# Matmul operand tiles moved to multiples of 1024 bytes, with a later first norm and a later sum for k

## The chip, the core and the metric

The kernel runs on one core of a Trainium2 chip. The metric is device time in microseconds (us) of one execution. A core has TensorE (PE; its weight loads are listed as PEld), VectorE (DVE), ScalarE (ACT), GpSimd (POOL) and a queue engine (SP) that issues most DMAs. TensorE multiplies a stationary tile by a moving tile of up to 512 columns and accumulates in PSUM. SBUF is the on-chip memory that holds both; an address here is a byte offset that is the same in each of its 128 partitions.

## The reference

One layer of a decoder trunk, for 256 tokens of width 2048, in float32:

```python
h = rmsnorm(x, norm_mix)
z = h @ w_in                      # 9472 columns, split into nine parts
hq, hf, hi, hgate, aq, ak, av, g_hg, g_at = jnp.split(z, offsets, axis=-1)
y_hg = (rmsnorm(hgrn2(hq, hf, hi, lower), hg_norm) * silu(hgate)) @ w_hg_out
qa, ka = rmsnorm(aq, q_norm), rmsnorm(ak, k_norm)      # per head
y_at = swa_sinks(qa, ka, av, sinks) @ w_at_out         # window 128
x = x + (sigmoid(g_hg) * y_hg + sigmoid(g_at) * y_at) @ w_out
h2 = rmsnorm(x, norm_ffn)
x = x + square(relu(h2 @ w_up)) @ w_down
```

## The kernel before

All weights are streamed once, as 250 chunks of 1 MiB (128 partitions x 2048 float32). A chunk is worked on in two halves, and the program is written as one long loop over half chunks, called ticks: tick 2i and 2i+1 belong to chunk i. The order of everything is written by hand: `at_pe(t, f)` and `at_post(t, f)` put f behind the main matmuls of tick t, `finish` puts an evacuation at a tick, and each engine executes its instructions strictly in the order in which the loop wrote them.

A float32 product is made of three products of rounded operands (`float32r`). For each half, ScalarE writes `hi`, the rounded copy of the chunk's half (`split_hi`, three ticks ahead), and VectorE writes `lo`, the remainder (`split_lo`, two ticks ahead). The activations have the same two parts. Two forms of half chunk follow:

- "one" (`mm_part`): 8 matmuls with hi stationary and both parts of an activation as 512 moving columns, then 8 with lo stationary and 256 moving columns. The input projection (activation `hT`; chunks 4 to 41, so 76 halves) and the up projection (`h2`; 64 chunks, 128 halves) have this form.
- "tok" (`mm_tok`): 12 matmuls with an activation stationary and 512 columns of hi or lo moving. The gates (32 chunks), the mixing (16), the output projection (16) and the down projection (64) have this form: 128 chunks of 24 matmuls, 3,072 in all.

The program starts with chunks 0 to 3 in quarters: 16 units of 4 + 4 matmuls (`start_split`, tiles `shi`/`slo`), fed by 1 MiB quarters of x (`xs`) and of the four chunks as they land. Behind these, SP's queue has x by tokens (`x_tok`, two DMAs of 1 MiB), chunk 4 (`raw4`), the constants, and chunks 5 and 6. ScalarE squares x by tokens with a running sum (`squares`), `norm_tok` makes the reciprocal root and two diagonal tiles `dg`, and TensorE sums them with ones into `rstd` (`norm_pe`, behind tick 9), which all evacuations of the input projection multiply by. Later `qknorm` norms q and k of the attention the same way: square, remainder (`nl`), a sum on TensorE (`nps`), a root. For k these are asked for from tick 68 on, the sum behind tick 70.

In the built program the first pool, `base`, holds small tiles of odd sizes and then the large ones, and all that follows is shifted by them. The tiles of the main matmuls begin at these places: `hT` (later `mixT` and half of `u`) at byte 21,472, which is 992 over a multiple of 1024; `xs` (later `oact` and the other half of `u`) also 992 over one; `raw`, `hi`, `lo`, `h2`, `shi`, `slo` all 32 over one. The identity in `consts`, the moving operand of every transpose, begins 384 over one. Every slice that a matmul moves or holds is a multiple of 512 bytes further on, and one of 512 columns is 2048 bytes long.

Of the kernel before, what the change touches and what calls it, by code (L numbers as in the profile page):

```python
# [10 lines left out]
F32 = mybir.dt.float32  # L11
# [7 lines left out]
P = 128  # L19
T = 256  # L20
# [22 lines left out]
def trunk_kernel(  # L43
# [14 lines left out]
    nc = tc.nc  # L58
    ctx.enter_context(tc.manual_schedule())

    base = ctx.enter_context(tc.tile_pool(name="base", bufs=1))
    raws = ctx.enter_context(tc.tile_pool(name="raws", bufs=4))
    split = ctx.enter_context(tc.tile_pool(name="split", bufs=3))
    ev = ctx.enter_context(tc.tile_pool(name="ev", bufs=2))
    psm = ctx.enter_context(tc.tile_pool(name="psm", bufs=4, space=PSUM))
    pss = ctx.enter_context(tc.tile_pool(name="pss", bufs=4, space=PSUM))

# [12 lines left out]
    S_END = len(chunks)  # L80
    AHEAD = 3
    N_START = 4
    T_START = 11
    START_LEAD = 4

    params = base.tile([P, P_W], F32, name="params")
    consts = base.tile([P, C_W], F32, name="consts")
    cr = base.tile([P, R_W], F32R, name="cr")
    rstd = base.tile([P, T], F32, name="rstd")
    lb = base.tile([P, HG_HEADS], F32, name="lb")  # L90
    omlb = base.tile([P, HG_HEADS], F32, name="omlb")
    kn8 = base.tile([P, 1], F32, name="kn8")

    ident = consts[:, C_ID : C_ID + P]
    ones = cr[:, R_ONES : R_ONES + P]
# [9 lines left out]
    def load(i):  # L105
        if i < S_END:
            raw_of[i] = raws.tile([P, KT, P], F32, tag="raw", name=f"raw{i}")
            nc.sync.dma_start(raw_of[i], chunks[i])
# [87 lines left out]
    def at_pe(s, f):  # L196
        pe_side.setdefault(s, []).append(f)

    def at_post(s, f):
        post.setdefault(s, []).append(f)  # L200
# [1 line left out]
    acts = {}  # L202

    def new_act(key, tag):
        acts[key] = base.tile([P, KT, 2, T], F32R, tag=tag, name=key)
        return acts[key]

    hT = new_act("hT", "A")

    xs = base.tile([P, KT, 2, T], F32, tag="C", name="xs")  # L210
    xv = xs[:, :, 0, :]
    xtok = xs[:, :, 1, :]

# [16 lines left out]
    def load_w(i, q):  # L230
        nc.sync.dma_start(raw0[i][:, 4 * q : 4 * q + 4, :], chunks[i][:, 4 * q : 4 * q + 4, :])
# [6 lines left out]
    for q in range(1, 4):  # L238
        load_x(4 * q, 4 * q + 4)
        for i in range(N_START):  # L240
            load_w(i, q)
    for t in range(2):
        nc.sync.dma_start(xtok[:, 8 * t : 8 * t + 8, :], x_tok[t].rearrange("p (m c) -> p m c", m=8))
    load(N_START)
    nc.sync.dma_start(cr0, csr)
    nc.sync.dma_start(consts, cst)
    load(N_START + 1)
    load(N_START + 2)

    def x_part(lo, hi):  # L250
# [44 lines left out]
        nc.tensor.matmul(ps, lhsT=lhsT, rhs=hi, start=True, stop=False)  # L295
        nc.tensor.matmul(ps, lhsT=lhsT, rhs=lo, start=False, stop=True)

    r1 = base.tile([P, 2], F32, name="r1")
    sm = base.tile([P, 3, 2], F32, name="sm")
    dg = base.tile([P, 2, 2, P], F32R, name="dg")  # L300

    def norm_tok(total_sq, r):
        v, q = sm[:, 1, :], sm[:, 2, :]
        nc.vector.tensor_scalar(v, total_sq, 1.0 / D, EPS, ALU.mult, ALU.add)
# [22 lines left out]
        part = xtok[:, 8 * t : 8 * t + 8, :]  # L327
        nc.scalar.activation(part, part, AF.Square, accum_out=sm[:, 0, t : t + 1])  # L328

    at_post(6, lower_bounds)  # L330
    at_post(6, lambda: squares(0))
    at_post(7, lambda: squares(1))
    at_post(7, constants)
    at_post(8, lambda: norm_tok(sm[:, 0, :], r1))
    at_pe(9, lambda: norm_pe("1"))
    at_post(10, lambda: norm_post("1"))

    evac = {}

# [296 lines left out]
    at_pe(2 * S_AV + 4, avpe)  # L636
    at_post(2 * S_AV + 5, avpost)

    def qknorm(s, z, gain, n, name):
        st = {}  # L640

        def new(m, dt=F32):
            return hg["pool"].tile([P, 512], dt, tag="g2", bufs=9, name=m)[:, 0:n]

        def a():
            sq, hi = st["sq"], st["hi"] = new(f"nq_{name}"), new(f"nh_{name}", F32R)
            nc.scalar.activation(hi, z, AF.Square)
            nc.gpsimd.tensor_mul(sq, z, z)

        def a2():  # L650
            st["lo"] = new(f"nl_{name}", F32R)
            nc.vector.tensor_sub(st["lo"], st["sq"], st["hi"].bitcast(F32))

        def b():
            st["ps"] = psum_side(f"nps_{name}")
            sums(st["ps"][:, 0:n], blk64, st["hi"], st["lo"])

        def c():
            st["v"] = mean_eps(st["ps"][:, 0:n], 64, new(f"nv_{name}"))

        def c2():
            st["r"] = rsqrt_start(st["v"], new, f"n{name}")

        def d():
            r = rsqrt_finish(*st["r"])
            nc.vector.scalar_tensor_tensor(z, z, gain, r, ALU.mult, ALU.mult)

        at_post(s, a)
        at_post(s + 1, a2)
        at_pe(s + 2, b)  # L670
        at_post(s + 3, c)
        at_post(s + 4, c2)
        at_post(s + 5, d)

    halves = (slice(0, 64), slice(64, P))

# [15 lines left out]
        for n, own in enumerate(halves):  # L692
            nc.vector.tensor_sub(t[halves[1 - n], n, :], aqz[own, j, :], t[own, n, :].bitcast(F32))

    qknorm(68, akz, kn8, T, "k")
    at_post(T_GATES, stack_k)
    for j, t in enumerate((74, 78, 82, 85)):
        qknorm(t, aqz[:, 2 * j : 2 * j + 2, :].rearrange("p j t -> p (j t)"), qng, 512, f"q{j}")
# [1 line left out]
    def pair(j, s):  # L700
# [20 lines left out]

        def a2():
            sc = pool().tile([P, 2, 384], F32, tag="sc", name=f"sc_{j}")
            mx = pool().tile([P, 2, 2], F32, tag="mx", name=f"mx_{j}")
            for n, h in enumerate(heads):
                nc.vector.scalar_tensor_tensor(
                    sc[:, n, :],
                    dist,
                    float(np.float32(2.0 ** (-8.0 * (h + 1.0) / AT_HEADS))),
                    st["ps"][n][:, 0:384],  # L730
                    ALU.mult,
                    ALU.add,
                )
            nc.vector.tensor_reduce(mx[:, :, 0:1], sc[:, :, 0:P], AX.X, ALU.max)
            nc.vector.tensor_reduce(mx[:, :, 1:2], sc[:, :, P:384], AX.X, ALU.max)
            for n, h in enumerate(heads):
                nc.vector.tensor_scalar(
                    mx[:, n, :], mx[:, n, :], params[:, P_SINK + h : P_SINK + h + 1], -1.0, ALU.max, ALU.mult
                )
            st.update(sc=sc, mx=mx)  # L740

        def b():
            sc, mx = st["sc"], st["mx"]
            sm = pool().tile([P, 2, 2], F32, tag="sm", name=f"sm_{j}")
            es = pool().tile([P, 2, 2], F32, tag="es", name=f"es_{j}")
            for n, h in enumerate(heads):
                for q, sl in enumerate((slice(0, P), slice(P, 384))):
                    nc.scalar.activation(
                        sc[:, n, sl], sc[:, n, sl], AF.Exp, bias=mx[:, n, q : q + 1], accum_out=sm[:, n, q : q + 1]
                    )  # L750
                nc.scalar.activation(es[:, n, :], mx[:, n, :], AF.Exp, bias=params[:, P_SINK + h : P_SINK + h + 1])
            st.update(sm=sm, es=es)
# [236 lines left out]
    for tick in range(2 * S_END + 2):  # L989
        i, odd = divmod(tick, 2)  # L990
        if not odd:
            if i >= N_START:
                load(i + AHEAD)
            for key, tag in fresh.get(i, ()):
                new_act(key, tag)
        if tick == 2 * N_START:
            to_hgrn()
        if tick == T_GATES:
            to_gates()
        if tick == 2 * S_OUT + 3:  # L1000
            open_ff()
        split_hi(ticks[tick + 3])
        split_lo(ticks[tick + 2])
        for f in due.pop(tick, ()):
            f()
        h = ticks[tick]
        i, odd = divmod(h, 2)
        if i < N_START:
            for n in (2 * tick, 2 * tick + 1):
                j, q = units[n]  # L1010
                if q == 0:
                    start_ps.append(psum_main(j) if j < 2 else psum_side(f"mm{j}"))
                mm_part(start_ps[j], hT, 4 * q, *start_w.pop(n), q == 0, q == 3)
                start_split(n + START_LEAD)
                if q == 3:
                    finish(jobs[j][2], 1, T_START + j // 2, start_ps[j], j)
        elif i < S_END:
            kind, act, ef = jobs[i][:3]
            if kind == "tok":
                k0, first, last = jobs[i][3:]  # L1020
                first, last = first and not odd, last and odd == 1
                if first:
                    main_ps["tok"] = [psum_main(f"{h}_{t}") for t in range(2)]
                ps = main_ps["tok"]
                mm_tok(ps, act(), k0 + 2 * odd, hi_of.pop(h), lo_of.pop(h), first, last)
            else:
                if not odd:
                    main_ps[i] = psum_main(h)
                ps = main_ps[i]
                mm_part(ps, act(), 8 * odd, hi_of.pop(h), lo_of.pop(h), not odd, odd == 1)  # L1030
            t0 = tick + 1 + 2 * (i in (S_FF, S_FF + 1))
            if i < N_START + 4:
                t0 = max(t0, T_START + i // 2)
            if S_G <= i < N_IN:
                t0 = max(t0, T_GATES + 1)
            finish(ef, odd, t0, ps, i)
        for f in post.get(tick, []):
            f()
        for f in pe_side.get(tick, []):
            f()  # L1040
# [98 lines left out]
```

## Time and profile before

| what | us |
|---|---|
| time, median of 3 runs (1372.82 to 1374.32) | 1372.89 |
| the profiled execution, its own time | 1372.77 |
| its span, first to last instruction | 1371.0 |
| TensorE busy in it | 1350.6 |
| VectorE busy | 852.0 |
| ScalarE busy | 686.3 |
| GpSimd busy | 188.6 |

Times inside the trace count from the span's start. A row of the timeline gives the start and the length of a run of equal instructions; matmuls overlap, so the pace of a series is read from the start of one run to the start of the next, not from the length of one matmul.

### The profile page before, as it was taken

The page shows a single profiled execution, that of the slowest core. Times are in us where ns is not written, and L with a number is a line of the kernel's source. Part 1 is how long each engine was busy: PE and PEld are TensorE (multiplying, and loading weights), DVE is VectorE, ACT ScalarE, POOL GpSimd, SP SyncE. Part 2 cuts the span into 40 slices and gives each one's busy share as a digit, 9 for nine tenths or more (in the row PEclk, how much of TensorE's full clock was granted, in tenths as well). Part 3 has the DMA queues.
Part 4 walks back from the last instruction along what each step waited for, and adds up shares of the span by engine and source line. Part 5 has one row for each costly group of instructions (what it writes and reads, how often), then busy time and mean ns, then how long its engine had stood idle before and what let it go on. Part 6 is the DMA issues. An engine that isn't in the chain of part 4 may idle for free.

```text
span 1371.0 us, 17892 instructions
## 1 busy us (share of the span) xinstructions
PE 1350.6 (99%) x6912; PEld 1140.1 (83%) x6912; DVE 852.0 (62%) x1067; ACT 686.3 (50%) x976; POOL 188.6 (14%) x181
## 2 busy tenths in 40 slices
PE   7999998999999999999999999999999999999998
PEld 6888887888888888888888888888888888888887
DVE  4688889795666466655666665444456666644443
ACT  5856656566665634454644444333344444443432
POOL 0334535310000001000111110000001111100000
PEclk9999999999999999999999999999999999999999
DMA  9554554455544555665555555555555555556661
GB/s 342 200 182 150 185 184 144 153 189 167 175 157 162 177 187 181 210 225 182 183 187 192 196 190 187 186 192 199 190 184 187 186 193 193 193 185 202 212 214 47
DMA packets 42453, 255.40 MB, mean 186 GB/s; under 512 B 4480, under 2 KB 8704, under 8 KB 12928
## 3 DMA queue, kind: packets, MB, share of 16 engines
q1 hardware_dynamic: 42224, 254.23, 54.1%
q8 instruction: 54, 0.88, 0.2%
q14 instruction: 31, 0.25, 0.1%
q10 hardware_dynamic: 144, 0.03, 0.0%
HBM read 252.15 MB, written 2.10 MB: 185 GB/s over the span
## 4 chain that ended last, share of the span: by engine, by line
PE 90%; DVE 4%; DMA 2%; issue 1%; POOL 1%; ACT 1%; SPq 0%; DVEq 0%; POOLq 0%; ACTq 0%
PE mm L129 23%; PE mm L153 17%; PE mm L151 17%; PE mm L152 17%; PE mm L137 12%; DMA raw<-w_in_t 1%; DVE lo L120 1%; DVE lf L418 1%; DMA xs<-xT 0%; POOL vT L342 0%; POOL lfb L404 0%; PE pt L767 0%; PE po L782 0%; PE s L713 0%; ACT xs L328 0%
## 5 line engine op out<-in xcount | busy, mean ns | idle before, releaser
L120 DVE TENSOR_TENSOR lo<-raw,hi 128x1024 fp32r<-128x1024 f32 x460 | 582.4, 1268 | 435.3 <-PE mm L152 266.4
L114 ACT CAST hi<-raw 128x1024 fp32r<-128x1024 f32 x460 | 482.5, 1050 | 608.8 <-PE mm L153 358.7
L129 PE MATMUL mm<-h,hi 128*128 128x512 f32 x1024 | 256.5, 392 | 0.0
L129 PEld LDWEIGHTS mm<-h,hi 128*128 128x128 f32 x1024 | 184.3, 189 | 33.1
L153 PE MATMUL mm<-hi,u 128*128 128x512 f32 x512 | 201.7, 394 | 0.0
L152 PE MATMUL mm<-lo,u 128*128 128x512 f32 x512 | 200.7, 392 | 0.0
L151 PE MATMUL mm<-hi,u 128*128 128x512 f32 x512 | 198.7, 388 | 0.0
L129 PE MATMUL mm<-hT,hi 128*128 128x512 f32 x608 | 156.3, 399 | 0.0
L137 PEld LDWEIGHTS mm<-h,lo 128*128 128x128 f32 x1024 | 139.7, 190 | 10.0
L137 PE MATMUL mm<-h,lo 128*128 128x256 f32 x1024 | 142.8, 282 | 0.0
L123 POOL CAST u<-s 128x256 fp32r<-128x256 f32 x64 | 60.3, 943 | 565.3 <-ACT s L930 565.3
L129 PEld LDWEIGHTS mm<-hT,hi 128*128 128x128 f32 x608 | 109.7, 189 | 21.0
L152 PEld LDWEIGHTS mm<-lo,u 128*128 128x128 f32 x512 | 96.1, 188 | 22.4
L151 PEld LDWEIGHTS mm<-hi,u 128*128 128x128 f32 x512 | 96.1, 188 | 21.4
L153 PEld LDWEIGHTS mm<-hi,u 128*128 128x128 f32 x512 | 96.3, 188 | 19.1
L151 PE MATMUL mm<-hi,hT 128*128 128x512 f32 x256 | 102.0, 398 | 0.0
L153 PE MATMUL mm<-hi,hT 128*128 128x512 f32 x256 | 100.7, 393 | 0.0
L152 PE MATMUL mm<-lo,hT 128*128 128x512 f32 x256 | 100.1, 391 | 0.0
L137 PEld LDWEIGHTS mm<-hT,lo 128*128 128x128 f32 x608 | 81.9, 190 | 8.3 <-DVE lo L120 1.5
L137 PE MATMUL mm<-hT,lo 128*128 128x256 f32 x608 | 83.3, 280 | 0.6 <-DVE lo L120 0.5
L151 PEld LDWEIGHTS mm<-hi,hT 128*128 128x128 f32 x256 | 48.1, 188 | 10.9 <-issue 1.4
L153 PEld LDWEIGHTS mm<-hi,hT 128*128 128x128 f32 x256 | 48.1, 188 | 10.3
(206 smaller groups left out, 1331.1 us busy)
## 6 DMA issues: line engine op xcount, KB each, us to landing
raw<-w_in_t SPq DMA_DIRECT2D x70, 1024.0 KB, 5.0
raw<-w_up_t SPq DMA_DIRECT2D x64, 1024.0 KB, 5.0
raw<-w_down_t SPq DMA_DIRECT2D x64, 1024.0 KB, 5.0
raw<-w_mix_t SPq DMA_DIRECT2D x16, 1024.0 KB, 4.9
raw<-w_out_t SPq DMA_DIRECT2D x16, 1024.0 KB, 5.0
raw<-w_in_t SPq DMA_DIRECT2D x16, 256.0 KB, 6.4
xs<-x_tok SPq DMA_DIRECT2D x2, 1024.0 KB, 10.4
x<-x_tok SPq DMA_DIRECT2D x8, 256.0 KB, 6.3
```

The lines of the kernel that those rows point to most:

```text
L114: nc.scalar.copy(hi, raw_of[i][:, 8 * q : 8 * q + 8, :])
L120: nc.vector.tensor_sub(lo, raw_of[i][:, 8 * q : 8 * q + 8, :], hi_of[h].bitcast(F32))
L123: copy(dst[..., 0, :], src)
L129: nc.tensor.matmul(ps, lhsT=hi[:, k, :], rhs=act[:, k0 + k, :, :].rearrange("p a t -> p (a t)"), start=(first and k == 0), stop=False,)
L137: nc.tensor.matmul(ps[:, T : 2 * T], lhsT=lo[:, k, :], rhs=act[:, k0 + k, 0, :], start=False, stop=(last and k == n - 1),)
L151: nc.tensor.matmul(ps[t], lhsT=xh, rhs=hi[:, k, :], start=(first and k == 0), stop=False)
L152: nc.tensor.matmul(ps[t], lhsT=xh, rhs=lo[:, k, :], start=False, stop=False)
L153: nc.tensor.matmul(ps[t], lhsT=xl, rhs=hi[:, k, :], start=False, stop=(last and k == 1))
L418: nc.vector.tensor_add(v[:, :, :, r], v[:, :, :, r], v[:, :, :, r - 1])
```

## The change

Three things change.

First, the layout. The large tiles leave `base` for a pool `big` that is opened first, behind a pad of 224 floats; `base` is opened after the weight pools, its tiles in another order and padded to 7 x 1024 bytes; `mx`, `sm` and `es` of the attention are widened to 128 bytes. In the built program `hT` begins at 17,408 and `xs` at 50,176, and with `raw`, `hi`, `lo`, `h2`, `shi`, `slo`, `dg`, `cr`, `consts` they all begin at multiples of 1024. No instruction changes its shape by this.

Second, the start. Chunks 4 and 5 are asked for ahead of x by tokens; the squares come one tick later, `lower_bounds` two ticks later and behind them, `norm_tok` one, the sum of `rstd` one (behind tick 10), and the evacuations of the first chunks one (`T_START` 12). Chunk 6 accumulates in a PSUM bank of the side pool, since the banks of chunks 0 and 1 are free one tick later.

Third, for k the sum on TensorE and what follows it come two ticks later.

```diff
-    base = ctx.enter_context(tc.tile_pool(name="base", bufs=1))
+    big = ctx.enter_context(tc.tile_pool(name="big", bufs=1))
+    big.tile([P, 224], F32, name="pad0")
     raws = ctx.enter_context(tc.tile_pool(name="raws", bufs=4))
     split = ctx.enter_context(tc.tile_pool(name="split", bufs=3))
     ev = ctx.enter_context(tc.tile_pool(name="ev", bufs=2))
+    base = ctx.enter_context(tc.tile_pool(name="base", bufs=1))
...
-    T_START = 11
+    T_START = 12
...
-    params = base.tile([P, P_W], F32, name="params")
-    consts = base.tile([P, C_W], F32, name="consts")
+    dg = base.tile([P, 2, 2, P], F32R, name="dg")
     cr = base.tile([P, R_W], F32R, name="cr")
     rstd = base.tile([P, T], F32, name="rstd")
+    consts = base.tile([P, C_W], F32, name="consts")
+    params = base.tile([P, 64], F32, name="params")[:, 0:P_W]
...
-        acts[key] = base.tile([P, KT, 2, T], F32R, tag=tag, name=key)
+        acts[key] = big.tile([P, KT, 2, T], F32R, tag=tag, name=key)
...
-    xs = base.tile([P, KT, 2, T], F32, tag="C", name="xs")
+    xs = big.tile([P, KT, 2, T], F32, tag="C", name="xs")
...
+    load(N_START)
+    load(N_START + 1)
     for t in range(2):
         nc.sync.dma_start(xtok[:, 8 * t : 8 * t + 8, :], x_tok[t].rearrange("p (m c) -> p m c", m=8))
-    load(N_START)
     nc.sync.dma_start(cr0, csr)
     nc.sync.dma_start(consts, cst)
-    load(N_START + 1)
     load(N_START + 2)
...
-    at_post(6, lower_bounds)
-    at_post(6, lambda: squares(0))
-    at_post(7, lambda: squares(1))
-    at_post(7, constants)
-    at_post(8, lambda: norm_tok(sm[:, 0, :], r1))
-    at_pe(9, lambda: norm_pe("1"))
-    at_post(10, lambda: norm_post("1"))
+    at_post(7, lambda: squares(0))
+    at_post(8, lambda: squares(1))
+    at_post(8, lower_bounds)
+    at_post(9, constants)
+    at_post(9, lambda: norm_tok(sm[:, 0, :], r1))
+    at_pe(10, lambda: norm_pe("1"))
+    at_post(11, lambda: norm_post("1"))
...
-    qknorm(68, akz, kn8, T, "k")
+    qknorm(68, akz, kn8, T, "k", late=2)
...
-                    main_ps[i] = psum_main(h)
+                    main_ps[i] = psum_side(f"mm{h}") if i == N_START + 2 else psum_main(h)
```

ScalarE at the start, from unit 13 to the sum's diagonal tiles. The number behind hi, lo and shi is the half chunk or unit, that behind raw the chunk. Before:

```order
L270 CAST shi13_302<-raw1_97 128x512
L114 CAST hi8_306<-raw4_123 128x1024
L270 CAST shi14_316<-raw2_98 128x512
L270 CAST shi15_328<-raw3_99 128x512
L114 CAST hi9_332<-raw4_123 128x1024
L287 ACTIVATE lb_79<-lb_79 128x8
L288 ACT_TABLE_LOAD
L328 ACTIVATE xs_83,sm_156<-xs_83 128x8x256
L114 CAST hi10_360<-raw5_127 128x1024
L328 ACTIVATE xs_83,sm_156<-xs_83 128x8x256
L114 CAST hi11_393<-raw5_127 128x1024
L305 ACTIVATE sm_156<-sm_156 128x2
```

The same stretch with the change:

```order
L276 CAST shi13_307<-raw1_105 128x512
L120 CAST hi8_311<-raw4_129 128x1024
L276 CAST shi14_321<-raw2_106 128x512
L276 CAST shi15_333<-raw3_107 128x512
L120 CAST hi9_337<-raw4_129 128x1024
L120 CAST hi10_357<-raw5_131 128x1024
L330 ACTIVATE xs_91,sm_88<-xs_91 128x8x256
L120 CAST hi11_388<-raw5_131 128x1024
L330 ACTIVATE xs_91,sm_88<-xs_91 128x8x256
L293 ACTIVATE lb_84<-lb_84 128x8
L294 ACT_TABLE_LOAD
L120 CAST hi12_417<-raw6_137 128x1024
```

The two squares of x by tokens (out xs,sm) now stand behind hi10 and hi11 instead of ahead of them, and the root of the norm (out sm alone) behind hi12. hi8 still stands ahead of shi14 and shi15.

TensorE at the sum for k (nps_k), near tick 70. mm70 and mm72 are chunks 35 and 36. Before:

```order
L137 MATMUL mm70_2327<-hT_82,lo70_2249 128x256 x8
L631 MATMUL avps_2346<-consts_76,avz_91 128x128 x2
L295 MATMUL nps_k_2349<-nh_k_2281,cr_77 128x256
L296 MATMUL nps_k_2349<-nl_k_2314,cr_77 128x256
L129 MATMUL mm70_2327<-hT_82,hi71_2247 128x512 x8
L137 MATMUL mm70_2327<-hT_82,lo71_2291 128x256 x8
```

The same stretch with the change:

```order
L143 MATMUL mm70_2332<-hT_90,lo70_2254 128x256 x8
L633 MATMUL avps_2351<-consts_82,avz_99 128x128 x2
L135 MATMUL mm70_2332<-hT_90,hi71_2252 128x512 x8
L143 MATMUL mm70_2332<-hT_90,lo71_2296 128x256 x8
L135 MATMUL mm72_2400<-hT_90,hi72_2294 128x512 x8
L143 MATMUL mm72_2400<-hT_90,lo72_2325 128x256 x8
L301 MATMUL nps_k_2417<-nh_k_2286,cr_80 128x256
L302 MATMUL nps_k_2417<-nl_k_2319,cr_80 128x256
```

The two small matmuls moved behind two more halves; nothing else changed its place on TensorE there.

## Rows read from the trace of the kernel before

**Rows 1.** The page, part 1: engine, busy us (share of the span), instructions.

```profile
PE 1350.6 (99%) x6912; PEld 1140.1 (83%) x6912; DVE 852.0 (62%) x1067; ACT 686.3 (50%) x976; POOL 188.6 (14%) x181
```

**Rows 2.** Timeline of TensorE, three stages: start, length, engine, line, operation, tiles, shapes.

```profile
47.96 2.02 PE L129 MATMUL mm<-hT,hi 128*128 128x512 f32 x8
49.82 1.07 PE L137 MATMUL mm<-hT,lo 128*128 128x256 f32 x8
50.73 0.62 PE L129 MATMUL mm<-hT,hi 128*128 128x512 f32 x2
...
702.49 2.00 PE L129 MATMUL mm<-h,hi 128*128 128x512 f32 x8
704.33 1.12 PE L137 MATMUL mm<-h,lo 128*128 128x256 f32 x8
...
724.84 2.00 PE L129 MATMUL mm<-h,hi 128*128 128x512 f32 x8
...
899.75 0.39 PE L151 MATMUL mm<-hi,u 128*128 128x512 f32 x1
...
904.55 0.39 PE L151 MATMUL mm<-hi,u 128*128 128x512 f32 x1
```

**Rows 3.** Timeline of TensorE behind its first long idle time.

```profile
34.54 1.91 PE L129 MATMUL mm<-hT,shi 128*128 128x512 f32 x4
36.25 1.05 PE L137 MATMUL mm<-hT,slo 128*128 128x256 f32 x4
```

**Rows 4.** Windows, TensorE: stretch, length, busy (matmuls), granted clock, DMA share, GB/s.

```profile
34.60:37.10 2.50, 2.50 (x9) 0.50 1.00 416
```

**Rows 5.** Timeline of TensorE, eight transposes of the output projection.

```profile
613.74 1.03 PE L890 MATMUL tr<-consts,x 128*128 128x128 f32 x8
```

**Rows 6.** Groups by line and form: count, busy us, mean ns, idle before.

```profile
L890 PE MATMUL tr<-consts,x 128*128 128x128 f32 x32 | 4.1, 272 | 0.0
```

**Rows 7.** Timeline of TensorE and ScalarE at the start; brackets: idle before, releaser.

```profile
29.22 0.62 PE L137 MATMUL mm<-hT,slo 128*128 128x256 f32 x4
32.87 1.20 PE L129 MATMUL mm<-hT,shi 128*128 128x512 f32 x4 [3.03 <-ACT shi L270]
...
45.18 2.02 PE L129 MATMUL mm<-hT,hi 128*128 128x512 f32 x8
...
31.25 1.04 ACT L114 CAST hi<-raw 128x1024 fp32r<-128x1024 f32 x1 [9.53 <-DMA raw<-w_in_t]
...
42.60 0.20 ACT L305 ACTIVATE sm<-sm 128x2 f32<-128x2 f32 x1
```

**Rows 8.** DMA issues of L243 (x_tok) and L108 (raw5, raw6), with landings.

```profile
L243 SPq DMA_DIRECT2D xs<-x_tok x2: 657/802/946, 15.8 to 16.5; - x2
DMA to landing us min/median/max: 8.6/10.4/12.2
...
L108 SPq DMA_DIRECT2D raw<-w_in_t x2: 430/430/430, 22.5 to 23.0; - x2
...
DMA to landing us min/median/max: 12.4/13.4/14.4
```

**Rows 9.** Timeline of TensorE and VectorE around the sum for k.

```profile
230.26 0.36 PE L295 MATMUL nps_k<-nh_k,cr 128*128 128x256 f32 x1
234.10 0.39 PE L296 MATMUL nps_k<-nl_k,cr 128*128 128x256 f32 x1 [3.47 <-DVE nl_k L652]
...
244.35 0.34 PE L489 MATMUL a<-qq,kk 128*64 128x64 f32 x4
...
231.90 1.21 DVE L120 TENSOR_TENSOR lo<-raw,hi 128x1024 fp32r<-128x1024 f32 x1
...
233.63 0.41 DVE L652 TENSOR_TENSOR nl_k<-nq_k,nh_k 128x256 fp32r<-128x256 f32 x1
...
238.85 0.68 DVE L466 TENSOR_TENSOR cross<-z,lf 128x256 f32<-128x256 f32 x1
```

**Rows 10.** Windows, VectorE, one of three like it.

```profile
122.00:146.00 24.00, 23.54 (x36) 1.00 0.46 153
```

More of the change, by code (lines that the diff above doesn't have):

```diff
@@ L82, in trunk_kernel @@
     N_START = 4
-    T_START = 11
+    T_START = 12
     START_LEAD = 4
-    params = base.tile([P, P_W], F32, name="params")
-    consts = base.tile([P, C_W], F32, name="consts")
+    dg = base.tile([P, 2, 2, P], F32R, name="dg")
     cr = base.tile([P, R_W], F32R, name="cr")
     rstd = base.tile([P, T], F32, name="rstd")
+    consts = base.tile([P, C_W], F32, name="consts")
+    params = base.tile([P, 64], F32, name="params")[:, 0:P_W]
     lb = base.tile([P, HG_HEADS], F32, name="lb")
     omlb = base.tile([P, HG_HEADS], F32, name="omlb")
-    kn8 = base.tile([P, 1], F32, name="kn8")
+    kn8 = base.tile([P, 8], F32, name="kn8")[:, 0:1]
+    r1 = base.tile([P, 8], F32, name="r1")[:, 0:2]
+    sm = base.tile([P, 4, 2], F32, name="sm")
+    base.tile([P, 24], F32, name="pad")
     ident = consts[:, C_ID : C_ID + P]
@@ L296, in sums @@
         nc.tensor.matmul(ps, lhsT=lhsT, rhs=lo, start=False, stop=True)
-    r1 = base.tile([P, 2], F32, name="r1")
-    sm = base.tile([P, 3, 2], F32, name="sm")
-    dg = base.tile([P, 2, 2, P], F32R, name="dg")
     def norm_tok(total_sq, r):
@@ L637, in trunk_kernel, with qknorm @@
     at_post(2 * S_AV + 5, avpost)
-    def qknorm(s, z, gain, n, name):
+    def qknorm(s, z, gain, n, name, late=0):
         st = {}
@@ L669, in qknorm @@
         at_post(s + 1, a2)
[L670 to L673, printed above, removed]
+        at_pe(s + 2 + late, b)
+        at_post(s + 3 + late, c)
+        at_post(s + 4 + late, c2)
+        at_post(s + 5 + late, d)
     halves = (slice(0, 64), slice(64, P))
@@ L723, in a2 @@
             sc = pool().tile([P, 2, 384], F32, tag="sc", name=f"sc_{j}")
-            mx = pool().tile([P, 2, 2], F32, tag="mx", name=f"mx_{j}")
+            mx = pool().tile([P, 2, 16], F32, tag="mx", name=f"mx_{j}")[:, :, 0:2]
             for n, h in enumerate(heads):
@@ L743, in b @@
             sc, mx = st["sc"], st["mx"]
-            sm = pool().tile([P, 2, 2], F32, tag="sm", name=f"sm_{j}")
-            es = pool().tile([P, 2, 2], F32, tag="es", name=f"es_{j}")
+            sm = pool().tile([P, 2, 16], F32, tag="sm", name=f"sm_{j}")[:, :, 0:2]
+            es = pool().tile([P, 2, 16], F32, tag="es", name=f"es_{j}")[:, :, 0:2]
             for n, h in enumerate(heads):
```

## The prediction

> **What bounds the kernel now.** I read the page first, then the timeline of TensorE by stages, then who made it wait. TensorE is busy 1350.6 of 1371.0 us [rows 1], so waits are worth 20 us at most, and anything larger must come from the pace of its matmuls. The pace is read from run to run. In the input projection a half chunk takes 50.73 - 47.96 = 2.77 us: 49.82 - 47.96 = 1.86 for eight matmuls of 512 columns (232.5 ns each) and 0.91 for eight of 256 (114 ns). In the up projection eight halves take 724.84 - 702.49 = 22.35, so 2.794 each: 1.84 (230 ns) and 0.954 (119 ns). In the down projection 21 matmuls take 904.55 - 899.75 = 4.80, 228.6 ns each [rows 2].
>
> What would it be with nothing in the way? Behind its first long idle time TensorE ran at a granted clock of 0.50, its lower level of 1.2 GHz [rows 4]; there four matmuls of 512 columns took 36.25 - 34.54 = 1.71 us, 427 ns each [rows 3], just one column per cycle. One column per cycle at 2.4 GHz is 213.3 ns for 512 and 106.7 for 256. So each main matmul costs 12 to 19 ns more than its columns at full clock, and nothing more at half clock: at full clock something feeds the array too slowly. The excess depends on where tiles lie: hT and h2 have the same shapes and weights at the same place, but hT begins at 992 and h2 at 32 over a multiple of 1024, and the 256-column matmuls differ by 5 ns, the 512-column ones by 2.5 the other way. Both places are 32 bytes off a multiple of 64. The only moving operand in the trace that is on one is the identity of the transposes: eight take 1.03 us with 0.272 for the last [rows 5, 6], so (1.03 - 0.27)/7 = 108.6 ns each, where 128 columns at two cycles are 106.7: 2 ns of excess. They read at half the rate, so this is only the nearest row.
>
> **The change part by part: the layout.** It removes no instruction; all it can do is change the pace. From 256 columns of hT (114 ns, 7 over) and of h2 (119, 13 over) and 512 of the down projection (15 over), the excess looks like one or two extra fetches of 64 bytes (16 columns, 6.7 ns) per 1024 bytes: what a read that starts 32 bytes off would need. On a multiple of 1024 these fetches go. I take what the transposes keep, 2 ns: 215.3 and 108.7 ns, so 8 x 324.0 = 2.592 us a half. Sum: up projection 128 x (2.794 - 2.592) = 25.9 us; input projection 76 x (2.77 - 2.592) = 13.5; the 3,072 matmuls of the token form x 13.3 ns = 40.9. Together 80.3. Bounds: with no excess left it is 2 ns x 6,336 matmuls = 12.7 more; if nothing goes, 0; if the new places are worse, a loss (below).
>
> On the price of an aligned matmul the Trainium skill (TensorE: Matmul & The Clock Gate, "Back-to-back issue gap") gives columns/2.4 + 2.5 ns at full clock, so 215.8 and 109.2, an estimate by which the layout would bring 77 us; no main matmul of this trace goes at that pace.
>
> Part of this is not kept. VectorE has three stretches, 122 to 146, 172 to 195 and 216 to 241.3, in which it is 98% busy [rows 10]: there TensorE lives on its lo tiles and cannot go faster. 72 us x 0.18/2.77 = 4.7; I take 5, with bounds 0 and 10, since from 270 to 300 VectorE is near that too. Elsewhere VectorE and ScalarE have room, and a chunk is asked for three chunks ahead. Layout: 75.
>
> **The start.** Now ScalarE stands 9.53 us at hi8, which waits for raw4, the DMA behind x by tokens; shi14 and shi15 of landed data stand behind it. TensorE, done with unit 13 at 29.22 + 0.46 = 29.68, idles 3.03 us and then runs at half clock for a while [rows 3, 4, 7]. Then it waits for the norm and takes up chunk 5 at 45.18, its second half ending at 50.73 [rows 2, 7]. With the change raw4 passes both x_tok DMAs. Those landed at 15.8 + 8.6 = 24.4 and 16.5 + 12.2 = 28.7 [rows 8], raw4 by 31.25; so 1 MiB of weights takes 2.5 us, the second x_tok 4.3, the first between these, and raw4 lands 6.8 to 8.6 earlier, near 23.5. hi8, shi14, shi15 are made before 29.68. TensorE goes on without a gap: two units (half a half-chunk each, 2.77 together) to 32.5, chunk 4 to 38.0, the first half of chunk 5 to 40.8. Now the norm. x_tok lands 2 x 2.5 later, at 29.4 and 33.7. On ScalarE the second square (2.0 us) ends at 35.7, then lb, a table load and hi12 (raw6 at 23.0 + 14.4 = 37.4 [rows 8], no earlier or later than now, as the same bytes go ahead of it) to 38.4. VectorE stands in lower_bounds until that square's lb, some 36, with lo11 (first needed at 43) queued behind it; then lo11 and the constants, to 39. The root then starts at 39.0 instead of 42.60, and TensorE resumes 45.18 - 42.60 = 2.58 behind it: 41.6. It waits 0.8 at most, ends chunk 5 at 44.4, and has won 50.73 - 44.4 = 6.3 us. Bounds: 6.9 without the wait, 3.3 with a norm 3 us later. With the faster pace TensorE only comes earlier to the same norm; 0.5 of the 6.3 is then already in the layout's sum: 5.8.
>
> The later evacuations, and chunk 6 in a side bank, I cost at nothing: the tick between them and group 0's chain hides them; without it, 1 us.
>
> **The sum for k.** TensorE reaches it at 230.26 and waits 3.47 for nl_k, which VectorE makes last thing in the third busy stretch; then it runs at half clock again, and from 230.26 to the a matmul at 244.35 go 14.09 us [rows 9]. With the change three halves and the two small matmuls stand there: 3 x 2.77 + 0.23 = 8.54. The first half's lo71 is ready at 231.90 + 1.21 = 233.11, where TensorE wants it at 230.26 + 1.86 = 232.12: 0.99 of new wait. So a at 239.8, with its last input, cross, ready at 238.85 + 0.68 = 239.5. Won: 4.5, bounds 3 and 5.5. nl_k, at 234.0, is two halves early.
>
> Sum from the profiled execution: 1371.0 - 75 - 5.8 - 4.5 = 1285.7 of span, 1.8 outside: **1287.5** (that execution, 1372.77, is the median of the runs shown).
>
> **The rivals.**
> (a) The excess is a fixed price per 1024-byte block that a moving slice touches: 512 columns from 32 or 992 touch three blocks, 15.3/3 = 5.1 ns each; 256 touch two, (116.5 - 106.7)/2 = 4.9. Moved to a multiple, each matmul touches one block fewer: 6,336 x 5.1 = 32 us, 30 behind VectorE. For it: it fits both sizes; against: hT and h2 differ. 1372.8 - 30 - 10.8 = 1332.
> (b) The layout brings nothing, as the excess belongs to reading four bytes a column at full clock. For it: no main matmul in the trace goes without; the transposes read at half the rate. Then start and k alone: 1362. The Trainium skill (SBUF — State Buffer, "Specifications (TRN2)") speaks for this: it knows lines of 16 bytes in SBUF, and every place before is already a multiple of 32, so by that rule the move does nothing; the trace's two paces for equal shapes do not agree with it.
> (c) Slower: what costs is moving and stationary tile at the same place over 1024. h2 with hi and lo (both at 32) pays 5.4 ns more per 256-column matmul than hT (992 against 32). After the change all pairs share their place: 3,072 + 608 matmuls x 5.4 = 20 us, less 10.8: 1382. It decides from 2.9 ns per matmul. Against: at 512 columns h2 is the faster.
>
> **How the numbers follow.** Forecast 0.52, (a) 0.18, (b) 0.20, (c) 0.07, else 0.03. The forecast's own range is 1276 (2 ns less) to 1306 (5 ns kept, or VectorE's 10). The range must reach (b), to leave out no more than 2 in 10: 1276 to 1364. A measurement of this kernel tells 0.2%, 2.7 us, from no change; only (c) is slower, and of (b) a little is the same, if start and k both fail: faster 0.90, same 0.03, slower 0.07.
>
> **What would show it.** Halves of 2.59 us in both projections and 215 ns in the token form for the forecast; 2.69 and 223.5 for (a); 2.77 and 228.6 for (b); over 231 for (c). No idle time of TensorE near 30 us, chunk 5 done near 44, granted clock 1.00 there and at the sum for k. Wrong if TensorE waits often for lo between 100 and 300 us, more than 10 us in all, or if the norm comes behind 45 us.

## The result, and the profile after

The changed kernel takes 1356.05 us (1355.38 to 1356.71), the kernel before 1372.86 (1372.18 to 1374.32): a ratio of 0.9876, 95% interval 0.9865 to 0.9888. It is faster by 16.8 us, where 85 were forecast. Its profiled execution took 1355.67 us with a span of 1353.9, so 17.1 of span are to be accounted for.

The page of the changed kernel, part 1 (engine, busy us, share of the span, instructions), beside [rows 1]:

```profile
PE 1341.0 (99%) x6912; PEld 1139.0 (84%) x6912; DVE 853.0 (63%) x1067; ACT 686.0 (51%) x976; POOL 193.6 (14%) x181
```

TensorE is still busy 99% of the span, and its busy time fell by 9.6 us only. The timeline of the changed kernel (start, length, engine, line, operation, tiles, shapes), first the half chunks from the first half of chunk 4 (31.60) to the first of chunk 6 (43.01), with the norm's sum (rstd) between the halves of chunk 5, then the sum for k:

```profile
31.60 2.00 PE L135 MATMUL mm<-hT,hi 128*128 128x512 f32 x8
...
37.19 2.00 PE L135 MATMUL mm<-hT,hi 128*128 128x512 f32 x8
...
39.98 0.28 PE L301 MATMUL rstd<-dg,cr 128*128 128x256 f32 x1
...
40.22 2.00 PE L135 MATMUL mm<-hT,hi 128*128 128x512 f32 x8
...
43.01 2.00 PE L135 MATMUL mm<-hT,hi 128*128 128x512 f32 x8
...
226.00 1.22 PE L143 MATMUL mm<-hT,lo 128*128 128x256 f32 x8 [0.69 <-DVE lo L126]
...
229.85 0.28 PE L301 MATMUL nps_k<-nh_k,cr 128*128 128x256 f32 x1
229.97 0.28 PE L302 MATMUL nps_k<-nl_k,cr 128*128 128x256 f32 x1
...
232.98 0.34 PE L491 MATMUL a<-qq,kk 128*64 128x64 f32 x4
```

**Start.** TensorE has no idle time between 29 and 45 us and no wait for the norm, and the half chunks follow each other at 2.79 us. The granted clock of this stretch was 1.00, its level of 2.4 GHz; before, it was 0.89 on average, with 0.50 behind the idle time [rows 3, 4]. Chunk 5 is done at 43.01 instead of 50.73 [rows 2]: 7.7 us. ScalarE shows why. Its timeline in the changed kernel (in brackets the idle time before and its releaser), beside [rows 7]:

```profile
22.97 1.05 ACT L120 CAST hi<-raw 128x1024 fp32r<-128x1024 f32 x1 [2.25 <-DMA raw<-w_in_t]
...
29.20 1.92 ACT L330 ACTIVATE xs<-xs 128x2048 f32<-128x2048 f32 x1 [1.34 <-DMA xs<-x_tok]
...
32.05 1.91 ACT L330 ACTIVATE xs<-xs 128x2048 f32<-128x2048 f32 x1
...
36.53 0.20 ACT L307 ACTIVATE sm<-sm 128x2 f32<-128x2 f32 x1
```

It waits 2.25 us for raw4 instead of 9.53, hi8 starts at 22.97 instead of 31.25, and the root of the norm at 36.53 instead of 42.60. **The sum for k** no longer waits for nl_k; of the 3.47 us [rows 9] 0.69 came back as a wait for a lo tile. The matmul a, which follows this sum, is at 232.98 instead of 244.35, so 11.4 us are won by then.

The rest, 5.7 us, is the pace: 6.0 won in the token form, less 0.3 lost in the input projection behind the matmul a. The groups of TensorE by line and form (count, busy us, mean ns of one; the mean includes the modelled drain, so only differences between means count), first of before, then of the changed kernel:

```profile
L129 PE MATMUL mm<-h,hi 128*128 128x512 f32 x1024 | 256.5, 392 | 0.0
L153 PE MATMUL mm<-hi,u 128*128 128x512 f32 x512 | 201.7, 394 | 0.0
L152 PE MATMUL mm<-lo,u 128*128 128x512 f32 x512 | 200.7, 392 | 0.0
L151 PE MATMUL mm<-hi,u 128*128 128x512 f32 x512 | 198.7, 388 | 0.0
L137 PE MATMUL mm<-h,lo 128*128 128x256 f32 x1024 | 142.8, 282 | 0.0
```

```profile
L135 PE MATMUL mm<-h,hi 128*128 128x512 f32 x1024 | 256.4, 392 | 0.0
L157 PE MATMUL mm<-hi,u 128*128 128x512 f32 x512 | 199.2, 389 | 0.0
L158 PE MATMUL mm<-lo,u 128*128 128x512 f32 x512 | 199.2, 389 | 0.0
L159 PE MATMUL mm<-hi,u 128*128 128x512 f32 x512 | 199.2, 389 | 0.0
L143 PE MATMUL mm<-h,lo 128*128 128x256 f32 x1024 | 142.8, 282 | 0.0
```

The up projection did not move at all (392 and 282 ns in both), although h2, hi and lo came to multiples of 1024. In the down projection the three operations, which had 394, 392 and 388 ns, all have 389: some 2.3 ns less on average. In start times (the first matmul of a stage to the first of the next) the token form won 2.6 us in gates, mix and output projection and 1.7 in each half of the down projection (175.79 before, 174.11 now, in the first), 6.0 together; the input projection lost about 0.02 us a half where it is not held up by VectorE, since hT (232.5 and 114 ns before) now has h2's pace (230 and 119). So: start 7.7, k 4.1 (4.3 at the matmul a, of which 0.2 go again in the next halves), token form 6.0, less some 0.7 in the input projection: 17.1.

### The profile page after: what moved, and what is told of

It is laid out like the page before. It is cut to its first block, busy times and chain, and to the rows that moved or that the text cites. A ratio compares the mean times of both kernels' runs of the same rounds, so it can differ in the third digit from the quotient of the medians.

```text
span 1353.9 us, 17891 instructions
## 1 busy us (share of the span) xinstructions
PE 1341.0 (99%) x6912; PEld 1139.0 (84%) x6912; DVE 853.0 (63%) x1067; ACT 686.0 (51%) x976; POOL 193.6 (14%) x181
## 4 chain that ended last, share of the span: by engine, by line
PE 91%; DVE 4%; POOL 2%; issue 1%; ACT 0%; DMA 0%; SPq 0%; DVEq 0%; POOLq 0%
PE mm L135 24%; PE mm L157 17%; PE mm L159 17%; PE mm L158 17%; PE mm L143 13%; DVE lo L126 2%; DVE lf L420 1%; POOL vT L344 0%; POOL lfb L406 0%; PE pt L769 0%; PE po L784 0%; DMA xs<-xT 0%; PE s L715 0%; DVE s L171 0%; PE mt L845 0%
## 5 line engine op out<-in xcount | busy, mean ns | idle before, releaser
L159 PEld LDWEIGHTS mm<-hi,hT 128*128 128x128 f32 x256 | 48.1, 188 | 10.3
```

Of the source, the lines that this page charges most:

```text
L159: nc.tensor.matmul(ps[t], lhsT=xl, rhs=hi[:, k, :], start=False, stop=(last and k == 1))
```

## The experiments

**Each part alone.** Two theories. The layout theory: start and k bring what was worked out, about 10.3, and the layout almost nothing but 2 ns in the token form. Its rival: the layout would bring much more, and something in the other two parts gives it back.

start_and_k, the layout of before with the other two parts:

```diff
-    T_START = 11
+    T_START = 12
...
+    load(N_START)
+    load(N_START + 1)
     for t in range(2):
...
-    qknorm(68, akz, kn8, T, "k")
+    qknorm(68, akz, kn8, T, "k", late=2)
...
```

> The old layout with the new start and the later sum for k. By the prediction's sums 6.3 + 4.5 = 10.8 us, so 1362.1; by the trace of the changed kernel 7.7 at chunk 5 and 4.3 at the sum for k, 12.0 and 1360.9. If the rest of the gain were an interaction with the layout, less than 9.

Measured: 1362.1 us, ratio 0.992 (0.9906 to 0.9933). Against the trace of before, chunk 5 is done 7.3 us earlier; 6.7 of these are left at the sum for k, 10.9 are won at the matmul a and 10.7 at the end. In this run TensorE took up chunk 4 earlier than in the changed kernel, at 31.01, and did wait for the norm:

```profile
40.05 0.39 PE L295 MATMUL rstd<-dg,cr 128*128 128x256 f32 x1 [0.56 <-ACT dg L312]
```

k_only:

```diff
...
-    qknorm(68, akz, kn8, T, "k")
+    qknorm(68, akz, kn8, T, "k", late=2)
```

> The later sum for k alone, all else as before: 4.5 us by the prediction, 4.3 by the trace of the changed kernel, so 1368.4 to 1368.6. Rival: VectorE's backlog gives the wait back at the next lo tile or at the a matmul, and less than 2 us are left.

Measured: 1368.8 us, ratio 0.9968 (0.9958 to 0.9978). Against the trace of before, 4.2 us are won from the sum for k to the matmul a, and 4.0 of them stay; the span is only 3.0 shorter, as chunk 5 was done 0.9 us later in this execution, where TensorE waited 3.10 us for the norm instead of 1.53. By medians the start is then worth 1368.8 - 1362.1 = 6.7 us.

layout_only, the changed kernel with the start and the sum for k of before, so that against the kernel before only the layout is new:

```diff
-    base = ctx.enter_context(tc.tile_pool(name="base", bufs=1))
+    big = ctx.enter_context(tc.tile_pool(name="big", bufs=1))
+    big.tile([P, 224], F32, name="pad0")
...
```

> The changed layout alone; order, loads and norms as before. By the trace of the changed kernel the token form wins 2.1 ns in each of 3,072 matmuls (6.0 us) and the halves of the input projection lose 0.02 us each where VectorE does not set the pace (0.5 us): 5.5 us faster, 1367.4. Theory that the layout matters only together with the new start (a matmul stream that begins elsewhere): no difference, 1372.9. My forecast's theory would have had 75 us.

Measured: 1365.37 us, ratio 0.9945 (0.9932 to 0.9957), 2 us less than expected. The token form brings 6.0 us and the input projection takes back 0.5, as in the changed kernel. The other 2.1 us come at the start: raw4 lands earlier here (hi8 starts at 29.09 us, in the trace of before at 31.25, in that of k_only at 30.67). Whether the places or the first loads' own spread did that isn't settled; where raw4 is asked for earlier it doesn't matter. So nothing is given back: the layout itself is worth 5.5 us.

**What the excess is.** A kernel with nothing of the layer, only series of 16 equal matmuls, each on another pair of places. Three lines of its table are

```python
# name, moving and stationary place in floats over 1024 bytes, moving and stationary columns, steps
("aa", 0, 0, 512, 128, 512, 128),
("ab", 8, 8, 512, 128, 512, 128),
("ac", 248, 8, 512, 128, 512, 128),
...
```

> This kernel computes nothing of the layer: it loads x, copies it into a moving and a stationary tile and runs series of 16 matmuls (each with its own weight load, 8 places each used twice) with nothing beside them on any engine, and each series has its own places, widths or type. What is told apart is where the 13 ns over the 213.3 ns of 512 columns, which the changed layout left in place, belong. Theory F (feeding four-byte columns at full clock costs one cycle in sixteen wherever the tile lies): about 227 ns for 512 columns and 113 for 256 in every fp32r series at its best place, the same with a stationary tile of 64 or 32 columns, 56.7 for 128 columns and 170 for 384; the two-byte series near 214 to 216 and 107 to 109. Theory W (each weight load takes time from the moving read): the excess falls to about half with a stationary tile of 64 columns and to a quarter with 32 (220 and 217 ns), and is as large for 256 columns as for 512. Theory P (my forecast's: a place off a multiple of 64 costs extra fetches): series at 32 or 992 bytes over a multiple of 1024 stand at 227 or more and those at a multiple at 215; the changed kernel speaks against it. For the place, theory R: only the distance between the moving and the stationary place counts, so the series with both at 0 and both at 32 agree, and the series with 992 against 32 is the faster one at 256 columns (114 against 119 ns) and the slower one at 512.

The timeline of that kernel (rows as above; the start of one series less that of the next is its 16 matmuls):

```profile
26.93 3.80 PE L83 MATMUL paa<-xr,wr 128*128 128x512 f32 x16
30.57 3.81 PE L83 MATMUL pab<-xr,wr 128*128 128x512 f32 x16
34.22 3.90 PE L83 MATMUL pac<-xr,wr 128*128 128x512 f32 x16
37.96 3.90 PE L83 MATMUL pad<-xr,wr 128*128 128x512 f32 x16
...
67.53 2.07 PE L83 MATMUL pba<-xr,wr 128*128 128x256 f32 x16
69.44 2.07 PE L83 MATMUL pbb<-xr,wr 128*128 128x256 f32 x16
71.35 2.00 PE L83 MATMUL pbc<-xr,wr 128*128 128x256 f32 x16
73.18 1.98 PE L83 MATMUL pbd<-xr,wr 128*128 128x256 f32 x16
...
95.38 3.84 PE L83 MATMUL pcd<-xr,wr 128*64 128x512 f32 x16
99.06 3.87 PE L83 MATMUL pce<-xr,wr 128*32 128x512 f32 x16
102.77 1.99 PE L83 MATMUL pcf<-xr,wr 128*64 128x256 f32 x16
```

With moving and stationary both at 0 (aa) 512 columns take 3.64/16 = 227.5 ns, both at 32 bytes (ab) 228.1, at 992 against 32 (ac) 233.8. For 256 columns it is the other way: 119.4 at 0 (ba) and at 32 (bb), 114.4 at 992 against 32 (bc). These are the paces of both kernels, without any other engine at work. No place brings 512 columns under 226.7 ns start to start. So theory P falls: a multiple of 1024 is no better than 32 bytes over one. Theory W falls too: with a stationary tile of 64 columns (cd) or 32 (ce) 512 columns take 230 and 232 ns, not 220 and 217. Of theory R both signs are there. Theory F has 227 and 113 ns as the best paces, but 128 moving columns took 111.6 ns where it wants 56.7.

More places for 256 columns, and steps of nothing from column to column:

```python
("eb", 0, 8, 256, 128, 512, 128),
...
("za", 0, 0, 512, 128, 0, 128),
...
if name == "za":
    rhs = x[:, 0:1].broadcast_to([P, 512])
```

> Again nothing of the layer: series of 16 matmuls with nothing beside them. First 256 moving columns at a multiple of 1024 with the stationary tile 0, 32, 64, 96 ... 992 bytes over one, and some the other way round; then 512 columns; then 512 columns that all read the same four bytes (step 0, series za) against the same 512 columns read each time (zb). Theory F (four-byte columns are fed at 16 columns in 17 cycles at full clock, and a weight load of 128 four-byte columns, which alone takes about 107 ns by the series with 128 moving columns, is only just hidden behind 256 columns): no place brings 512 columns below 226.7 or 256 below 113.3; step 0 is no faster than zb if the array or its feed is the limit, and falls to about 216 if the reads from memory are. Theory R (the two reads disturb each other by their distance): at 256 columns the distances 0, 256 and 512 stand near 119 to 120 and some distances of 32 to 96 near 114; at 512 columns the other way, 227 at 0, 256 and 512 and 230 to 234 between.

Measured: with all 512 columns reading the same four bytes (za) 218.7 ns, where the other series of 512 keep 226.7 to 234. Of 256 columns none with a full stationary tile fell under 116.6 ns here, and the pair (992, 32), which settled at 113.3 in the series above, took 117.8. The two kernels have their tiles at the same addresses and differ in the series only: at 256 columns the place alone doesn't settle the pace, and what ran before is all that is left to differ.

A last kernel of this kind steps the columns apart:

```python
...
rhs = x[:, m + 512 * j : m + 512 * j + cols * step : step]
...
```

> Nothing of the layer: the output is only some sums of the input, so the total says nothing. Nineteen series of 16 equal matmuls (the first of 48), start to start in the trace. Theory of the feed (a four-byte moving column cannot be read at one per cycle for long: the excess goes with the bytes that the moving rows span, not with their place): 512 fp32r columns side by side 226.7 ns; at a step of 8 or 16 bytes far slower (at a step of 8 over 400 ns, if whole lines are read); all columns from one element 219 ns; two-byte columns side by side 215.8, at any place, but two-byte columns at a step of 4 bytes 226.7 as the four-byte ones. Rival (the excess belongs to the four-byte type in the array, not to the reading): steps of 8 and 16 bytes leave 226.7 ns, two-byte columns stay at 215.8 with a step of 4 bytes. Transposes of 128 four-byte columns with the identity at 0, at 32 and at 992 (weights at 32): 108 to 109 ns at every place by the feed theory, as they take a column every second cycle, so they could not have shown what a place costs; a difference of 3 ns or more between places would mean that they were a fair proxy.

Its timeline (ga, gb, gc: four-byte columns 4, 8 and 16 bytes apart; gd all from one element; gf, gg, gh: two-byte columns 2, 4 and 8 bytes apart; ha to hd: transposes with the identity at 0, 32, 992, 0 and the stationary tile at 0, 0, 32, 64; of gf's 16 matmuls the trace lacks one):

```profile
26.50 3.79 PE L91 MATMUL pga<-xr,wr 128*128 128x512 f32 x16
30.12 7.41 PE L91 MATMUL pgb<-xr,wr 128*128 128x512 f32 x16
37.35 7.56 PE L91 MATMUL pgc<-xr,wr 128*128 128x512 f32 x16
44.73 3.68 PE L91 MATMUL pgd<-xr,wr 128*128 128x512 f32 x16
48.25 3.81 PE L91 MATMUL pge<-xr,wr 128*128 128x512 f32 x16
51.90 3.63 PE L91 MATMUL pgf<-xb,wb 128*128 128x512 bf16 x15
55.36 3.78 PE L91 MATMUL pgg<-xb,wb 128*128 128x512 bf16 x16
58.98 7.38 PE L91 MATMUL pgh<-xb,wb 128*128 128x512 bf16 x16
...
73.11 1.91 PE L86 MATMUL pha<-idt,wf 128*128 128x128 f32 x16
74.86 1.91 PE L86 MATMUL phb<-idt,wf 128*128 128x128 f32 x16
76.60 1.91 PE L86 MATMUL phc<-idt,wf 128*128 128x128 f32 x16
78.35 1.91 PE L86 MATMUL phd<-idt,wf 128*128 128x128 f32 x16
```

Four bytes a column: 3.62/16 = 226 ns; eight: 452; sixteen: 461; one element for all: 220. Two-byte columns side by side take 216, but four bytes apart 226 and eight bytes apart 451, as the four-byte ones do. So next to nothing hangs on the type; what counts is how far the columns lie apart. Nor is it the amount of memory: 64 columns side by side, read eight times over (ge), settle at 226.7 too. That settles it for the bulk: of the 13.4 ns over 213.3 at equal places **10.9 go with reading one column every four bytes** (226.7 against 215.8), whatever the place; the last 2.5 are there with two-byte columns as well. Two-byte columns side by side stood at 215.8 to 215.9 at the other two pairs of places tried too (496 against 16 bytes, 0 against 32), so no cost of the place was seen with them.

The Trainium skill (TensorE: Matmul & The Clock Gate, "Back-to-back issue gap") gives columns/2.4 + 2.5 ns for a matmul by itself at full clock, an estimate of 215.8 for 512; the two-byte series agrees (216), the four-byte ones don't (226.7). The Trainium skill (SBUF — State Buffer, "Specifications (TRN2)") wants two hits in a line of 16 bytes for full bandwidth; the measurement differs, as two columns in 16 bytes (gb) went at half pace, 452 ns.

The transposes take (74.86 - 73.11)/16 = 109 ns at each of four pairs of places: they could not have shown what a place costs. Plain matmuls of 128 four-byte columns, each with its own stationary tile, take 111.6 ns as well (ch in pace_places), so it isn't even shown that the moving read is what limits a transpose.

**What the places do.** Two theories: what counts is the distance between the moving and the stationary place, or it is the absolute place (a multiple of 1024 is good). pace_patterns runs the two forms as the kernel does, six halves to a series:

```python
# name, form, places of the activations, of hi and of lo in floats over 1024 bytes, order
("oa", "one", 0, 0, 0, 0),
("ob", "one", 248, 8, 8, 0),
("oc", "one", 8, 8, 8, 0),
...
("oe", "one", 240, 0, 0, 0),
...
```

> Nothing of the layer: the output is only some sums of the input, so the total says nothing. Twenty series of main matmuls in the kernel's own order, six halves each: the form of the projections (8 of 512 columns on hi, 8 of 256 columns on lo) and the form of the token products (three of 512 columns, the weights moving), with the tiles at different places over a multiple of 1024 bytes. Measured: time of one half (start to start, 16 or 12 matmuls). Theory of the distance (what counts is how far the moving place lies from the stationary place): projection form with all tiles at 0 or all at 32 bytes 2.797 us a half as in the changed kernel, weights 64 bytes behind the activations (992 against 32, or 0 against 64) 2.771 as in the input projection of the kernel before; token form with all at 0 or all at 32 12 x 226.8 ns = 2.72 us, at a distance of 64 bytes 12 x 229 = 2.75 or more. Theory of the absolute place (multiples of 1024 are what helps): all at 32 as slow in the token form as 992 against 32 (2.75 or more), and 0 against 64 between. If hi at 0 and only lo moved keeps 227 ns for 512 columns and gives 113 ns for 256, a half of the projection form takes 2.74 us and the series names a place worth trying in the kernel; if the slow locking of the 256-column matmuls (120 ns) comes from the 512-column ones ahead of them, no place of lo changes it.

The first row of series of the projections' form in its timeline:

```profile
35.06 2.00 PE L83 MATMUL poa<-act,hr 128*128 128x512 f32 x8
...
51.81 2.03 PE L83 MATMUL pob<-act,hr 128*128 128x512 f32 x8
...
68.46 1.99 PE L83 MATMUL poc<-act,hr 128*128 128x512 f32 x8
...
85.20 2.02 PE L83 MATMUL pod<-act,hr 128*128 128x512 f32 x8
...
101.84 2.02 PE L83 MATMUL poe<-act,hr 128*128 128x512 f32 x8
```

All at 0 (oa): 16.75/6 = 2.79 us a half. 992 against 32 (ob): 2.775. All at 32 (oc): 2.79. 0 against 64 (od): 2.773. So equal places are alike wherever they lie, and so are the three with the weights 64 bytes ahead of the activations (oe: 960 against 0, 2.78, and 2.773 from its third half on). In the token form: all at 0 226.8 ns, all at 32 226.8 too (after its first half), 992 against 32 228.9, 0 against 64 228.9. Moving lo alone (64 bytes: 2.78; other places up to 2.807) or taking hi and lo by turns (2.773 at best) brought no half below 2.76. In the token form, lo alone moved by 64 bytes (te) is worse than hi and lo both moved: 232 ns. So the distance of a matmul's own two tiles is not the whole rule; what is multiplied before and behind it counts too.

In the layer, all_32 shifts every tile by 32 bytes, and weights_64 shifts hi and lo, with all that is laid out behind them (h2 too), by 64:

```diff
-    big.tile([P, 224], F32, name="pad0")
+    big.tile([P, 232], F32, name="pad0")
```

```diff
     split = ctx.enter_context(tc.tile_pool(name="split", bufs=3))
+    split.tile([P, 16], F32, tag="pad", bufs=1, name="padw")
```

> The changed kernel with 32 bytes more ahead of everything: all tiles of main matmuls, moving and stationary, lie 32 bytes over a multiple of 1024. Distance theory: the time of the changed kernel, 1356 us within 1.5, token form 226.8 ns a matmul, projections 2.797 us a half. Absolute-place theory: the layout's gain is lost, 1361 to 1362 us or more, token form 229 ns.

> The changed kernel with hi and lo (and the small tiles behind them) 64 bytes over a multiple of 1024, hT, mixT, oact and u left at multiples; h2 moves with the weights (64 against 64). So the distance between weights and activations is that of the kernel before, and the activations alone are at multiples. Distance theory: the layout's gain is undone, token form 229 ns or more (3,072 x 2.2 ns = 6.8 us more), input projection back to 2.771 us a half (about 1 us less): 1361 to 1363 us; if the distance seen with 0 against 64 in a row of equal matmuls (233 ns) shows here in full, 3,072 x 6.5 ns = 20 us more, 1375. Absolute-place theory: the token form's activations are still at multiples, so it keeps at least half of its gain, 1356 to 1359 us.

Measured: all_32 1356.49 us (1356.0 to 1356.54), ratio to before 0.9878 (0.9863 to 0.9893), the time of the changed kernel, with no main tile at a multiple of 64. weights_64 1361.38 us (1361.04 to 1362.23), 0.9915 (0.9899 to 0.9932), with all activations of the token form still at multiples of 1024. Its groups are those of before to the tenth:

```profile
L160 PE MATMUL mm<-hi,u 128*128 128x512 f32 x512 | 201.7, 394 | 0.0
L159 PE MATMUL mm<-lo,u 128*128 128x512 f32 x512 | 200.7, 392 | 0.0
L158 PE MATMUL mm<-hi,u 128*128 128x512 f32 x512 | 198.7, 388 | 0.0
```

The up projection, whose two tiles moved together, kept its 392 and 282 ns. The absolute place falls; how far the two tiles lie apart stands. In the kernel before that was 64 bytes for hT, oact, mixT and u (992 against 32) and none for h2 (32 against 32), which is why h2 went at another pace than hT, and kept it when both tiles came to multiples of 1024.

**A version from this.** The projections' form likes the 64 bytes, the token form the equal places. h2 is used in the projections' form only, so it alone is moved:

```diff
+        p.tile([P, 240], F32, name="padh")
         acts["h2"] = p.tile([P, KT, 2, T], F32R, name="h2")
```

> The changed kernel with 960 bytes more ahead of h2, so that h2 lies at 960 over a multiple of 1024, 64 bytes from the place of hi and lo, and hT, mixT, oact, u, hi and lo stay at multiples. By the row of the pattern series (960, 0, 0): 2.773 us a half of the up projection in place of 2.794, 128 halves, 2.7 us less: 1353.4 us, and nothing else moves; this would beat both kernels. Rival (the projections' pace in the layer is set by something other than the distance, such as writes of other engines into the same memory): no change from the changed kernel, 1356.0.

Measured: 1353.82 us (1353.34 to 1353.98), ratio to before 0.9858 (0.9842 to 0.9875); the changed kernel had 1355.38 to 1356.71. Groups of the up projection:

```profile
L135 PE MATMUL mm<-h,hi 128*128 128x512 f32 x1024 | 259.2, 395 | 0.0
L143 PE MATMUL mm<-h,lo 128*128 128x256 f32 x1024 | 137.5, 277 | 0.0
```

The 512 columns take 3 ns more than in the changed kernel, the 256 columns 5 less: 2.5 us by start times over the two up projections, where 2.7 were expected. The intervals of the two ratios overlap, but no run of either kernel reaches into the range of the other.

## Why the prediction was wrong

The sign and the mechanisms of two parts were right; the layout, 75 of the 85 us forecast, was wrong, and the time lies in the wide range only because that reached to the rivals.

- **The layout, the step that failed:** "On a multiple of 1024 these fetches go. I take what the transposes keep, 2 ns". Two paces for equal shapes were read as extra fetches of a read that starts 32 bytes off, and so the whole excess of 12 to 19 ns was put down to the place. What the runs showed: of the 13.4 ns over at 512 columns at equal places 10.9 belong to reading a column every four bytes (226.7 at 0 as at 32, 215.8 with two-byte columns), none goes on a multiple of 1024, and on top of that other distances between the two tiles cost 0 to 8 ns. The transposes were named as only the nearest row; pace_steps shows that they have 109 ns whatever the place, so they were no evidence for a price of the place. Of 80.3 us the layout brought 5.5.
- **The row that spoke against it** was there: h2 with hi and lo at the same place, 230 and 119 ns [rows 2], is the pair that the change made of all the others. Taking it as the pace to come would have given 119 ns for the input projection, about 0.02 us a half lost, and left the token form as the one unknown. The prediction used this pair in rival (c), for a loss at 256 columns, and didn't carry it to the sum.
- **VectorE's stretches** (5 us of the layout not kept) had nothing to limit, as TensorE didn't get faster there.
- **The start** was 5.8 in the sum, 6.3 by itself. It measured 7.7 in the trace and 6.7 by medians. raw4 (hi8 at 22.97, "near 23.5") and the first square (29.20, x_tok "at 29.4") were right. The root came at 36.53, not 39.0: the second x_tok was there when ScalarE was free for it at 32.05 (33.7 was worked out), and raw6 when it came to hi12 at 35.57 (37.4 was worked out). So the wait of 0.8 us for the norm didn't come in this run; in start_and_k, where the root came at 38.09, it did, with 0.56. And TensorE took up chunk 4 at 31.60, not at 32.5. That 0.9 is no gain of the change but the spread of the first loads (quarters of x of 512 KB and of chunks of 256 KB): with the same order of work the same half starts at 32.46 in all_32, where chunk 5 is done 6.9 us earlier than before, and at 31.01 in start_and_k. So the step was right, and its 6.3 lies just below what the runs spread over, 6.7 to 7.7. The signs named for it came: no idle time near 30 us, chunk 5 done at 43.01, a granted clock of 1.00 there and at the sum for k.
- **The sum for k** was 4.5 and measured 4.2 to 4.3 at the matmul a in three traces, of which 4.0 to 4.1 stay, with the foreseen wait for lo at 0.69 instead of 0.99.
- **The rivals.** (b), the excess belongs to reading four bytes a column, is what the runs bear out for the bulk: 1362 was its time, and start_and_k, without the layout, has 1362.1. None of them had the 2 ns of the token form, which is what lies between 1362 and 1356. (a) wanted 223.5 ns at multiples of 1024 and 32 us; the series have 226.7 there and at 32 over one alike. (c), equal places cost 5.4 ns, holds for 256 columns alone and is turned round for 512.

## What to carry to other kernels

Before a stall-free engine's pace is put down to where tiles lie, look for the pair in the trace that already lies as the change would have it, and take its pace; a row of another kind of instruction is a proxy only if it is limited by the same thing. Compare places as pairs (moving against stationary), not one by one, and ask for each form of matmul apart: here one form wins from a shift from which the other loses. A part that moves a load ahead of a wait can be worked out from the landings of the trace to within 0.4 to 1.4 us here; such sums hold better than one price times six thousand.

## What the runs showed of the hardware

- Four-byte columns side by side feed the array at 226.7 ns for 512, two-byte ones at 215.8; four-byte columns eight or sixteen bytes apart, and two-byte ones eight apart, cost 0.88 to 0.90 ns each.
- On top, 512 four-byte columns pay 0 to 8 ns by the distance between moving and stationary place: none at 0, 256 or 512 bytes (226.7 ns), 5 at 128 (232), 6.6 at 32 and mostly at 64 (233.3), 7.6 at 96 (234.3). The distance doesn't fix it wholly: 64 against 0 took 229 to 230, 32 against 992 233, both with the moving tile 64 bytes ahead. What causes it is open. The reading of the next stationary tile beside the moving one could: for it, 256 columns with a stationary tile of 64 columns take 113.2 to 113.3 ns at equal places where one of 128 takes 120; against it, at 512 columns the narrow one takes 229.9 against 226.7.
- After each change from 256 to 512 columns the first five matmuls of 512 take 228 to 236 ns before 226.7 is reached, at equal places; so a half of the projections' form at equal places isn't the sum of two steady paces, 8 x 226.7 + 8 x 120 ns = 2.77 us, but 2.79.
